# Ordered level products, decay rows written by GpSimd, and equal statistics tiles in a two-layer hybrid of attention and gated linear attention

## The chip, the cores and the metric

One core of one Trainium2 chip runs the whole kernel. The metric is device microseconds of one execution, from the first to the last instruction with the little that lies around them. Less is better.

## What is computed

Two layers, each a feed-forward block, a token mixer and a second feed-forward block, all with a root-mean-square norm before and after, over 16 meta tokens and 256 sequence tokens (272 columns) of width 1024. In the second layer the meta tokens are dropped after the mixer's keys and values.

```python
for l in range(DEPTH):
    h = h + 0.5 * rmsnorm(swiglu(rmsnorm(h, g_pre_ffn1[l]), w_ffn1_gu[l], w_ffn1_down[l]), g_post_ffn1[l])
    mix = token_mixer(rmsnorm(h, g_pre_mix[l]), ...)
    h = h + rmsnorm(mix, g_post_mix[l])
    h = h + 0.5 * rmsnorm(swiglu(rmsnorm(h, g_pre_ffn2[l]), w_ffn2_gu[l], w_ffn2_down[l]), g_post_ffn2[l])

# in the mixer, attention with a forget gate (8 heads of 64)
s = q @ k.T * scale + cum[q] - cum[k];  p = softmax(where(allowed, s, -inf));  o = p @ v
# in the mixer, gated linear attention (4 heads, keys of 64, values of 128)
att[t, s] = sum_k q[t, k] * k[s, k] * exp(cb[t, k] - cb[s, k])   # s <= t, in blocks of 128
```

Here `cum` and `cb` are running sums of log gates along the tokens.

## The kernel before, in words

Activations lie transposed: 128 partitions of features, 272 columns of tokens. Each weight block (128x1024, fetched by SyncE) is split by ScalarE (`wh`, line 106) and VectorE (`wl`, line 112) into a rounded part and a rest, and each 128x128 piece gives three products of 272 columns (`mm3`, lines 122 to 124), one after another on TensorE. These products fill the program. A scheduler that simulates the program sets the order of instructions on every engine, within the program's dependencies; the mixer spreads its small work over the 41 projection blocks by a table (`at(i, function)`).

Four places matter here.

**Statistics.** `inv_rms` (lines 164 to 186) gives one over the root mean square of every token, as a row that is the same on all 128 partitions. Squares are summed over features by products with a column of ones (line 171), tokens in tiles of 128, 128 and 16 (of 128 and 128 where meta tokens are gone); VectorE scales the sums in one operation for the full tiles and one for the rest (line 179); GpSimd raises them to the power of minus one half (line 180); TensorE turns the columns back into a row by full products with the identity (line 183). `prep` calls it while products go on: five times with 272 columns, once with 256. `Post.done` calls it between two blocks, where TensorE has nothing else: four times with 272 columns, once with 256. There 5 and then 8 products whose result nobody reads (`idle`, line 161) fill TensorE's wait.

**Decay rows.** `decays` (from line 396) makes the running sums `cf` of the eight attention heads. The scores are products of 104 rows: 64 of the head, rows 64 to 72 and 96 to 104 for the two sums, and zeros between, which GpSimd writes once a layer (lines 344 and 345). `qa` has ones marks in 64 to 72 and `cf` in 96 to 104, `ka` has `-cf` and marks; the sums come by two DMAs on ScalarE's queue (lines 421 and 422), the marks by two on GpSimd's (lines 346 and 347).

**Scores.** `scores(b)` (line 645) makes two heads' scores in two products each; `meta_scores` (line 694) those of the meta tokens.

**Level products.** Gated linear attention is summed over seven levels (64, 32, ..., 1). `level` makes decayed keys and queries `E`, `products` multiplies them per head. Heads 0 and 2 lie on partitions 0 to 63, heads 1 and 3 on 64 to 127 (`r` is the half). For levels of 16 and less a head has two products of 128 stationary columns (line 562), and in the first layer, for levels of 8 and less, a third of 16 stationary columns for the meta tokens (line 565):

```python
for hd in range(GH):
    r, hh = hd % 2, hd // 2
    x = head_rows(E, hd)
    for k in range(2):
        nc.tensor.matmul(pp[r][...], x[:, o : o + P], second(x[:, o : o + P], L), ...)
    if meta:
        nc.tensor.matmul(pp[r][:META, ...], x[:, :META], second(x[:, :META], L), ...)
```

`diagonal` (lines 588 and 590) has the same form with 128 and 16 columns. A product of 32-bit operands shows as two rows in the trace, a transposition as one.

Of the kernel before, what the change touches and what calls it, by code (L numbers as in the profile page):

```python
# [9 lines left out]
F32 = mybir.dt.float32  # L10
# [3 lines left out]
ALU = mybir.AluOpType  # L14
AX = mybir.AxisListType

P = 128
META = 16
SEQ = 256
NT = META + SEQ  # L20
D = 1024
# [27 lines left out]
def hybrid_kernel(ctx: ExitStack, tc: tile.TileContext, xT, w_in, w_al, w_fg, w_o, w_gu1, w_dn1, w_gu2, w_dn2, w_end, g_end, vecs, consts, marks, out):  # L49
# [22 lines left out]
    ms = cp.tile([P, 4], F32, name="ms")  # L72
    nc.gpsimd.memset(ms, 1.0)
# [90 lines left out]
    def inv_rms(parts, n, factor, warm=False):  # L164

        tt = [(o, min(P, n - o)) for o in range(0, n, P)]
        J = len(tt)
        st = bank("po")
        for i, part in enumerate(parts):
            for j, (o, m) in enumerate(tt):  # L170
                last = nc.tensor.matmul(st[:m, j : j + 1], part[:, o : o + m], one, start=i == 0 and j == 0,
                                 stop=i == len(parts) - 1, skip_group_check=True)
        if warm:
            idle(last, WARM[0])
        rp = sp.tile([P, 4], F32, tag="rp", name="rp")
        q = 1.0 / (factor * factor)
        for m, a, b in ((P, 0, n // P), (n % P, n // P, J)):
            if m and b > a:
                nc.vector.tensor_scalar(ms[:m, a:b], st[:m, a:b], q / D, q * EPS, ALU.mult, ALU.add)
        nc.gpsimd.tensor_tensor(rp[:, :J], ms[:, :J], nhalf[:, :J], ALU.pow)  # L180
        bc = bank("po")
        for j, (o, m) in enumerate(tt):
            last = nc.tensor.matmul(bc[:, o : o + m], rp[:m, j : j + 1].broadcast_to([m, P]), ident[:m, :m], start=True, stop=True)  # L183
# [156 lines left out]
    def operands():  # L340

        qa = cp.tile([P, FH, NT], F32, tag="qa", name="qa")
        ka = cp.tile([P, FH, NT], F32, tag="ka", name="ka")
        nc.gpsimd.memset(qa[64:96], 0.0)
        nc.gpsimd.memset(ka[64:96], 0.0)
        nc.gpsimd.dma_start(qa[64:72], marks)
        nc.gpsimd.dma_start(ka[96:104], marks)
        return qa, ka

    def mixer(l, xh, xl, rs, qa, ka, c0):  # L350
# [6 lines left out]
        with tc.tile_pool(name="mix", bufs=1) as mp, tc.tile_pool(name="tmp", bufs=2) as tp:  # L357
# [39 lines left out]
            def decays():  # L397
# [17 lines left out]
                cf = a[32:40, 2, :]  # L415
                nc.vector.tensor_tensor_scan(cf, one[32:40].broadcast_to([8, NT]), b[32:40, 2, :], 0.0, ALU.mult, ALU.add)
                for f in range(2):
                    nc.vector.tensor_tensor_scan(G[:, f, :], one.broadcast_to([P, NT]), b[:, f, :], 0.0, ALU.mult, ALU.add)
                nf = sm[32:40]
                nc.vector.tensor_scalar(nf, cf, -1.0, None, ALU.mult)  # L420
                nc.scalar.dma_start(qa[96:104], cf.unsqueeze(1).broadcast_to([8, FH, NT]))
                nc.scalar.dma_start(ka[64:72], nf.unsqueeze(1).broadcast_to([8, FH, NT]))
# [108 lines left out]

            def products(i):
# [23 lines left out]
                for hd in range(GH):  # L556
                    r, hh = hd % 2, hd // 2
                    x = head_rows(E, hd)
                    for k in range(2):
                        o = TILES[k + 1][0]  # L560
                        q = 2 * k + hh
                        nc.tensor.matmul(pp[r][:, q * 64 : q * 64 + 64].rearrange("p (b l) -> p b l", l=L), x[:, o : o + P],  # L562
                                         second(x[:, o : o + P], L), start=True, stop=True)
# [13 lines left out]
            def diagonal():  # L577
# [4 lines left out]
                for hd in range(GH):  # L582
                    r, hh = hd % 2, hd // 2
                    xk, xq = head_rows(gk, hd), head_rows(gq, hd)
                    for k in range(2):
                        o = TILES[k + 1][0]
                        q = 2 * k + hh
# [354 lines left out]
```

## Time and profile before

| what | value |
|---|---|
| median of three runs | 1270.57 us (1266.27 to 1270.88) |
| the profiled execution | 1268.24 us |
| its span, first to last instruction | 1266.4 us |
| TensorE busy | 1247.4 us, 99% |
| VectorE busy | 893.4 us, 71% |
| ScalarE busy | 697.5 us, 55% |
| GpSimd busy | 34.9 us, 3% |
| TensorE's granted clock | 0.997 of full speed |

In the trace's rows PE is TensorE, DVE is VectorE, ACT is ScalarE, POOL is GpSimd and SP is SyncE. L122 is line 122 of the kernel, `out<-in` are the program's tile names. Ends of TensorE's rows are modelled and overlap the next row, so what a product costs is read from the start of one row to the start of the next.

### The profile page before, as it was taken

The page shows a single profiled execution, that of the slowest core. Times are in us where ns is not written, and L with a number is a line of the kernel's source. Part 1 is how long each engine was busy: PE and PEld are TensorE (multiplying, and loading weights), DVE is VectorE, ACT ScalarE, POOL GpSimd, SP SyncE. Part 2 cuts the span into 40 slices and gives each one's busy share as a digit, 9 for nine tenths or more (in the row PEclk, how much of TensorE's full clock was granted, in tenths as well). Part 3 has the DMA queues.
Part 4 walks back from the last instruction along what each step waited for, and adds up shares of the span by engine and source line. Part 5 has one row for each costly group of instructions (what it writes and reads, how often), then busy time and mean ns, then how long its engine had stood idle before and what let it go on. Part 6 is the DMA issues. An engine that isn't in the chain of part 4 may idle for free.

```text
span 1266.4 us, 25250 instructions
## 1 busy us (share of the span) xinstructions
PE 1247.4 (99%) x9826; PEld 1210.2 (96%) x9826; DVE 893.4 (71%) x1831; ACT 697.5 (55%) x1451; POOL 34.9 (3%) x43
## 2 busy tenths in 40 slices
PE   7999999999999999999999999999999999999997
PEld 7999999988999999999999999999898999999986
DVE  6777655887567787776568777558986687877662
ACT  7555544764555565554446555446755554755551
POOL 2000000000000100000000000001000000000000
PEclk9999999999999999999999999999999999999999
DMA  9655555443245636556536555564434564665650
GB/s 307 203 171 170 166 175 158 153 119 100 88 138 176 178 126 184 172 170 169 177 114 212 172 178 161 168 192 134 138 96 122 161 185 155 200 187 182 181 166 34
DMA packets 58198, 203.87 MB, mean 161 GB/s; under 512 B 6688, under 2 KB 8000, under 8 KB 58048
## 3 DMA queue, kind: packets, MB, share of 16 engines
q1 hardware_dynamic: 57376, 201.19, 51.7%
q8 instruction: 77, 1.26, 0.4%
q10 hardware_dynamic: 576, 0.80, 0.3%
q14 instruction: 41, 0.34, 0.1%
q0 software_dynamic: 128, 0.28, 0.1%
HBM read 200.92 MB, written 1.05 MB: 159 GB/s over the span
## 4 chain that ended last, share of the span: by engine, by line
PE 82%; issue 14%; DMA 1%; ACT 1%; POOL 0%; SPq 0%; ACTq 0%; DVE 0%; DVEq 0%; POOLq 0%
PE mm L122 13%; PE mm L124 12%; PE mm L123 12%; PE pp L122 7%; PE pp L124 7%; PE pp L123 7%; PE s L122 5%; PE s L123 5%; PE s L124 5%; PE pp L562 1%; PE s L161 1%; PE s L645 1%; DMA w<-in_w_gu 1%; PE po L183 1%; DMA ka<-sm 1%
## 5 line engine op out<-in xcount | busy, mean ns | idle before, releaser
L106 ACT CAST wh<-w 128x512 fp32r<-128x512 f32 (+1 forms) x768 | 464.6, 613 | 414.9 <-PE mm L123 183.8
L112 DVE TENSOR_TENSOR wl<-w,wh 128x512 fp32r<-128x512 f32 (+1 forms) x768 | 516.2, 681 | 246.4 <-ACT wh L106 231.0
L122 PE MATMUL mm<-xh,wh 128*128 128x272 f32 (+1 forms) x1072 | 309.4, 291 | 9.6 <-ACT wh L106 8.7
L124 PE MATMUL mm<-xh,wl 128*128 128x272 f32 (+1 forms) x1072 | 308.8, 289 | 0.0
L123 PE MATMUL mm<-xl,wh 128*128 128x272 f32 (+1 forms) x1072 | 307.8, 288 | 0.0
L122 PEld LDWEIGHTS mm<-xh,wh 128*128 128x128 f32 x1072 | 201.7, 189 | 11.7 <-ACT wh L106 8.9
L123 PEld LDWEIGHTS mm<-xl,wh 128*128 128x128 f32 x1072 | 202.9, 189 | 1.2 <-issue 0.9
L124 PEld LDWEIGHTS mm<-xh,wl 128*128 128x128 f32 x1072 | 202.2, 189 | 1.6 <-issue 1.1
L124 PE MATMUL s<-xh,wl 128*128 128x272 f32 (+1 forms) x496 | 142.2, 287 | 0.0
L123 PE MATMUL s<-xl,wh 128*128 128x272 f32 (+1 forms) x496 | 142.0, 287 | 0.0
L122 PE MATMUL s<-xh,wh 128*128 128x272 f32 (+1 forms) x496 | 141.0, 288 | 0.0
L124 PE MATMUL pp<-xh,wl 128*128 128x272 f32 (+1 forms) x480 | 137.2, 289 | 0.0
L123 PE MATMUL pp<-xl,wh 128*128 128x272 f32 (+1 forms) x480 | 137.0, 288 | 0.0
L122 PE MATMUL pp<-xh,wh 128*128 128x272 f32 (+1 forms) x480 | 134.0, 289 | 0.0
L123 PEld LDWEIGHTS s<-xl,wh 128*128 128x128 f32 x496 | 93.4, 188 | 0.1
L124 PEld LDWEIGHTS s<-xh,wl 128*128 128x128 f32 x496 | 93.4, 188 | 0.0
L122 PEld LDWEIGHTS s<-xh,wh 128*128 128x128 f32 x496 | 92.8, 188 | 0.1
L123 PEld LDWEIGHTS pp<-xl,wh 128*128 128x128 f32 x480 | 90.9, 189 | 0.0
L124 PEld LDWEIGHTS pp<-xh,wl 128*128 128x128 f32 x480 | 90.8, 190 | 0.0
L122 PEld LDWEIGHTS pp<-xh,wh 128*128 128x128 f32 x480 | 89.3, 190 | 0.0
L122 PE MATMUL pp<-hh,wh 128*128 128x272 f32 x264 | 76.1, 288 | 0.0
L122 PE MATMUL mm<-hh,wh 128*128 128x272 f32 x264 | 76.1, 288 | 0.0
(291 smaller groups left out, 2123.9 us busy)
## 6 DMA issues: line engine op xcount, KB each, us to landing
w<-in_w_gu SPq DMA_DIRECT2D x175, 512.0 KB, 3.6
w<-in_w_in SPq DMA_DIRECT2D x82, 512.0 KB, 3.6
w<-in_w_dn SPq DMA_DIRECT2D x48, 512.0 KB, 3.5
w<-in_w_end SPq DMA_DIRECT2D x22, 512.0 KB, 4.0
w<-in_w_dn SPq DMA_DIRECT2D x24, 384.0 KB, 3.5
w<-in_w_fg SPq DMA_DIRECT2D x16, 512.0 KB, 3.6
w<-in_w_o SPq DMA_DIRECT2D x16, 512.0 KB, 3.6
h<-in_xT SPq DMA_DIRECT2D x8, 136.0 KB, 4.7
```

The costliest lines, as they stand in the source:

```text
L106: i = nc.scalar.copy(wh[:, :n], w[:, a:b])
L112: nc.vector.tensor_tensor(wl[:, :n], w[:, a:b], wh[:, :n].bitcast(F32), ALU.subtract)
L122: nc.tensor.matmul(o, a, x[0], start=start, stop=False)
L123: nc.tensor.matmul(o, a, x[1], start=False, stop=False)
L124: nc.tensor.matmul(o, b, x[0], start=False, stop=stop)
L161: m = nc.tensor.matmul(o[:, :P], ident, ident, start=True, stop=True)
L183: last = nc.tensor.matmul(bc[:, o : o + m], rp[:m, j : j + 1].broadcast_to([m, P]), ident[:m, :m], start=True, stop=True)
L562: nc.tensor.matmul(pp[r][:, q * 64 : q * 64 + 64].rearrange("p (b l) -> p b l", l=L), x[:, o : o + P], second(x[:, o : o + P], L), start=T ...
L645: nc.tensor.matmul(s[:, c : c + e], qa[:104, hd, q0:e], ka[:104, hd, 0:e], start=True, stop=True)
```

## The change

Products of all heads come first, alternating between the partition halves, the narrow meta ones last and with 128 stationary columns in place of 16 (112 of the resulting rows are not read). The running sums go into the scores once only: `ka` gets `cf` in rows 64 to 72 by a GpSimd copy out of the scan's result, `qa` has marks of minus one, and scores have 72 rows. The term of the query's own sum is left out, which a softmax along keys does not see. The zero rows, their GpSimd writes, one marks DMA, the negation on VectorE and both DMAs on ScalarE's queue go. `inv_rms` cuts 272 tokens into four tiles of 68, scales with one VectorE operation, and turns back by transpositions.

```diff
     def inv_rms(parts, n, factor, warm=False):
-        tt = [(o, min(P, n - o)) for o in range(0, n, P)]
-        J = len(tt)
+        m = P if n % P == 0 else n // 4
+        tt = range(0, n, m)
...
-        for m, a, b in ((P, 0, n // P), (n % P, n // P, J)):
-            if m and b > a:
-                nc.vector.tensor_scalar(ms[:m, a:b], st[:m, a:b], q / D, q * EPS, ALU.mult, ALU.add)
-        nc.gpsimd.tensor_tensor(rp[:, :J], ms[:, :J], nhalf[:, :J], ALU.pow)
+        nc.vector.tensor_scalar(ms[:m, :J], st[:m, :J], q / D, q * EPS, ALU.mult, ALU.add)
+        nc.gpsimd.tensor_tensor(rp[:m, :J], ms[:m, :J], nhalf[:m, :J], ALU.pow)
         bc = bank("po")
-        for j, (o, m) in enumerate(tt):
-            last = nc.tensor.matmul(bc[:, o : o + m], rp[:m, j : j + 1].broadcast_to([m, P]), ident[:m, :m], start=True, stop=True)
+        for j, o in enumerate(tt):
+            last = nc.tensor.transpose(bc[:, o : o + m], rp[:m, j : j + 1].broadcast_to([m, P]), ident[:m, :m])
...
     def operands():
-        nc.gpsimd.memset(qa[64:96], 0.0)
-        nc.gpsimd.memset(ka[64:96], 0.0)
         nc.gpsimd.dma_start(qa[64:72], marks)
-        nc.gpsimd.dma_start(ka[96:104], marks)
...
                 for rows, f0, f1 in parts:
                     nc.vector.tensor_tensor(b[rows, f0:f1, :], b[rows, f0:f1, :], a[rows, f0:f1, :], ALU.subtract)
-                cf = a[32:40, 2, :]
-                nc.vector.tensor_tensor_scan(cf, one[32:40].broadcast_to([8, NT]), b[32:40, 2, :], 0.0, ALU.mult, ALU.add)
+                    if f0 == 2:
+                        cf = a[rows, 2, :]
+                        nc.vector.tensor_tensor_scan(cf, one[rows].broadcast_to([8, NT]), b[rows, 2, :], 0.0, ALU.mult, ALU.add)
+                        nc.gpsimd.tensor_copy(ka[64:72], cf.unsqueeze(1).broadcast_to([8, FH, NT]))
...
-                nf = sm[32:40]
-                nc.vector.tensor_scalar(nf, cf, -1.0, None, ALU.mult)
-                nc.scalar.dma_start(qa[96:104], cf.unsqueeze(1).broadcast_to([8, FH, NT]))
-                nc.scalar.dma_start(ka[64:72], nf.unsqueeze(1).broadcast_to([8, FH, NT]))
...
+            def both_halves(ks):
+                return [(k, hh, r) for k in range(ks) for hh in range(2) for r in range(2)]
...
-                    if meta:
-                        nc.tensor.matmul(pp[r][:META, 256 + hh * 8 : 264 + hh * 8].rearrange("p (b l) -> p b l", l=L),
-                                         x[:, :META], second(x[:, :META], L), start=True, stop=True)
+                for _, hh, r in both_halves(meta):
+                    x = E[64 * r : 64 * r + 64, hh]
+                    nc.tensor.matmul(pp[r][:, 256 + hh * 8 : 264 + hh * 8].rearrange("p (b l) -> p b l", l=L),
+                                     x[:, :P], second(x[:, :META], L), start=True, stop=True)
...
-                        nc.tensor.matmul(s[:, c : c + e], qa[:104, hd, q0:e], ka[:104, hd, 0:e], start=True, stop=True)
+                        nc.tensor.matmul(s[:, c : c + e], qa[:72, hd, q0:e], ka[:72, hd, 0:e], start=True, stop=True)
```

How the scheduler's order moves is shown at three places; a row's `x2` is two instructions of that form. First TensorE at a level's products in the first layer (the level of 1; `E_4141` are its operands, `pp_4194` and `pp_4195` the banks of the two halves), before:

```order
L124 MATMUL mm_4155<-xh_2755,wl_4073 128x272
L562 MATMUL pp_4194<-E_4141 128x64 x2
L565 MATMUL pp_4194<-E_4141 16x8
L562 MATMUL pp_4195<-E_4141 128x64 x2
L565 MATMUL pp_4195<-E_4141 16x8
```

and the end of the same level now:

```order
L558 MATMUL pp_4194<-E_4141 128x64
L558 MATMUL pp_4195<-E_4141 128x64
L562 MATMUL pp_4194<-E_4141 128x8
L562 MATMUL pp_4195<-E_4141 128x8
...
L120 MATMUL mm_4221<-xh_2755,wh_4133 128x272
L121 MATMUL mm_4221<-xl_2756,wh_4133 128x272
```

The two pairs of rows came twice before, a narrow product behind every two wide ones of a head; now eight wide ones come in alternation and four narrow ones behind them.

Second, GpSimd from the statistics before the first layer's mixer to the mixer's end (`rp` are powers in `inv_rms`, `ss` powers of the mixer's own norm), before:

```order
L443 MEMSET vm_3002 128x32
L180 TENSOR_TENSOR rp_2736<-ms_73,nhalf_75 128x3
L180 TENSOR_TENSOR rp_2824<-ms_73,nhalf_75 128x3
L748 TENSOR_TENSOR ss_4415<-ss_4415,nhalf_75 16x4
L748 TENSOR_TENSOR ss_4518<-ss_4518,nhalf_75 128x4
```

and now:

```order
L436 MEMSET vm_3004 128x32
L177 TENSOR_TENSOR rp_2736<-ms_2735,nhalf_73 68x4
L177 TENSOR_TENSOR rp_2826<-ms_2825,nhalf_73 68x4
L413 COPY ka_155<-lsa_3072 8x2176
L744 TENSOR_TENSOR ss_4415<-ss_4415,nhalf_73 16x4
L744 TENSOR_TENSOR ss_4518<-ss_4518,nhalf_73 128x4
```

The copy of 2176 elements a partition stands between the powers; the next operation in GpSimd's queue belongs to the mixer's end.

Third, TensorE at the first two heads' scores in the first layer (`mm_3333` is the block of values of heads 2 and 3, `mm_3390` the block behind it), before:

```order
L122 MATMUL mm_3333<-xh_2755,wh_3234 128x272
L123 MATMUL mm_3333<-xl_2756,wh_3234 128x272
L124 MATMUL mm_3333<-xh_2755,wl_3235 128x272
L645 MATMUL s_3254<-ka_155,qa_154 128x144
L645 MATMUL s_3254<-ka_155,qa_154 128x272
L645 MATMUL s_3261<-ka_155,qa_154 128x144
L645 MATMUL s_3261<-ka_155,qa_154 128x272
L122 MATMUL mm_3333<-xh_2755,wh_3238 128x272
```

and now:

```order
L122 MATMUL mm_3390<-xh_2755,wl_3309 128x272
L545 MATMUL pp_3378<-E_3327 64x64 x2
L545 MATMUL pp_3379<-E_3327 64x64 x2
L641 MATMUL s_3254<-ka_155,qa_154 128x144
L641 MATMUL s_3254<-ka_155,qa_154 128x272
L641 MATMUL s_3261<-ka_155,qa_154 128x144
L641 MATMUL s_3261<-ka_155,qa_154 128x272
```

The scores stood in the middle of the block `mm_3333`, after 68 products of 272 columns behind the decays' own (line 402); now they stand after 102 of them, behind the next block and inside the products of the level of 64.

## Rows read from the trace of the kernel before

**Rows 1.** The page, busy time of each engine: busy us (share of the span) xinstructions.

```profile
PE 1247.4 (99%) x9826; PEld 1210.2 (96%) x9826; DVE 893.4 (71%) x1831; ACT 697.5 (55%) x1451; POOL 34.9 (3%) x43
```

**Rows 2.** Timeline of PE, a level's products, first layer: start, us, what.

```profile
325.08 0.29 PE L124 MATMUL mm<-xh,wl 128*128 128x272 f32 x1
325.30 0.66 PE L562 MATMUL pp<-E 64*128 64x64 f32 x4
325.89 0.20 PE L565 MATMUL pp<-E 64*16 64x8 f32 x2
...
328.41 0.28 PE L123 MATMUL mm<-xl,wh 128*128 128x272 f32 x1
```

**Rows 3.** Timeline of PE, a level's products, second layer.

```profile
917.31 0.29 PE L124 MATMUL mm<-xh,wl 128*128 128x272 f32 x1
917.53 1.16 PE L562 MATMUL pp<-E 64*128 64x64 f32 x16
...
918.84 0.28 PE L123 MATMUL mm<-xl,wh 128*128 128x256 f32 x1
```

**Rows 4.** Timeline of PE, the diagonal's products, first layer, then second.

```profile
331.18 0.29 PE L124 MATMUL mm<-xh,wl 128*128 128x272 f32 x1
...
334.75 0.29 PE L123 MATMUL mm<-xl,wh 128*128 128x272 f32 x1
...
963.03 0.28 PE L124 MATMUL mm<-xh,wl 128*128 128x256 f32 x1
...
964.66 0.28 PE L123 MATMUL mm<-xl,wh 128*128 128x256 f32 x1
```

**Rows 5.** Timeline of PE, statistics inside running products: sums, then the turning back.

```profile
20.30 0.29 PE L122 MATMUL mm<-xh,wh 128*128 128x272 f32 x1
...
21.21 0.29 PE L124 MATMUL mm<-xh,wl 128*128 128x272 f32 x1
...
24.60 0.29 PE L124 MATMUL pp<-xh,wl 128*128 128x272 f32 x1
...
25.81 0.29 PE L123 MATMUL pp<-xl,wh 128*128 128x272 f32 x1
```

**Rows 6.** Timeline of all engines, between two blocks: sums scaled, power, turning back.

```profile
650.43 0.21 DVE L179 TENSOR_SCALAR ms<-po 128x2 f32<-128x2 f32 x2 [0.37 <-PE po L171]
650.81 0.85 POOL L180 TENSOR_TENSOR rp<-ms,nhalf 128x3 f32<-128x3 f32 x1 [186.76 <-DVE ms L179]
...
651.72 1.03 PE L183 MATMUL po<-con,rp 128*128 128x128 f32 x6
...
652.68 2.05 PE L161 MATMUL s<-con 128*128 128x128 f32 x16
```

**Rows 7.** Groups by line: shapes xcount, busy us, mean ns, idle before.

```profile
L748 POOL TENSOR_TENSOR ss<-ss,nhalf 128x4 f32<-128x4 f32 x4 | 4.0, 1007 | 125.3 <-DVE ss L747 125.3
L345 POOL MEMSET ka<- 32x2176 f32 x2 | 3.8, 1912 | 52.3 <-PE pp L124 52.3
```

**Rows 8.** Waits of PE: who, for whom, us in total, times, longest.

```profile
PE s L645 <- DMA ka<-sm: 2.1, 2, 1.1
PE mm L122 <- DVE ka L436: 0.9, 2, 0.6
```

**Rows 9.** Timeline of DVE at the first layer's decays.

```profile
248.43 0.71 DVE L416 TENSOR_TENSOR_SCAN lsa<-ones,lsb 8x272 f32<-8x272 f32 x1
...
249.93 0.29 DVE L420 TENSOR_SCALAR sm<-lsa 8x272 f32<-8x272 f32 x1
...
251.78 1.34 DVE L418 TENSOR_TENSOR_SCAN G<-ones,lsb 128x272 f32<-128x272 f32 x2
```

**Rows 10.** Busy us of each engine, 250 to 260 us.

```profile
250.00:260.00 10.00, 8.62 (x63) 7.93 (x61) 9.84 (x25) 6.86 (x16) 0.00 (x0) 1.00 0.54 164
```

**Rows 11.** Timeline of DVE and POOL where a power meets subtractions.

```profile
232.49 1.87 DVE L112 TENSOR_TENSOR wl<-w,wh 128x512 fp32r<-128x512 f32 x3
232.70 2.38 POOL L180 TENSOR_TENSOR rp<-ms,nhalf 128x3 f32<-128x3 f32 x1 [16.95 <-DVE ms L179]
```

More of the change, by code (lines that the diff above doesn't have):

```diff
@@ L71, in hybrid_kernel @@
     one = ones[:, 0:1]
-    ms = cp.tile([P, 4], F32, name="ms")
-    nc.gpsimd.memset(ms, 1.0)
     nhalf = cp.tile([P, 4], F32, name="nhalf")
@@ L555, in products @@
                 mask = con[:, C_LVL + i * P : C_LVL + (i + 1) * P].bitcast(I32)
[L556 to L563, printed above, removed]
-                    if meta:
-                        nc.tensor.matmul(pp[r][:META, 256 + hh * 8 : 264 + hh * 8].rearrange("p (b l) -> p b l", l=L),
-                                         x[:, :META], second(x[:, :META], L), start=True, stop=True)
+                for k, hh, r in both_halves(2):
+                    x = E[64 * r : 64 * r + 64, hh]
+                    o = TILES[k + 1][0]
+                    q = 2 * k + hh
+                    nc.tensor.matmul(pp[r][:, q * 64 : q * 64 + 64].rearrange("p (b l) -> p b l", l=L), x[:, o : o + P],
+                                     second(x[:, o : o + P], L), start=True, stop=True)
+                for _, hh, r in both_halves(meta):
+                    x = E[64 * r : 64 * r + 64, hh]
+                    nc.tensor.matmul(pp[r][:, 256 + hh * 8 : 264 + hh * 8].rearrange("p (b l) -> p b l", l=L),
+                                     x[:, :P], second(x[:, :META], L), start=True, stop=True)
                 for r in range(2):
@@ L581, in diagonal @@
                 mask = con[:, C_LVL + i * P : C_LVL + (i + 1) * P].bitcast(I32)
[L582 to L587, printed above, removed]
-                        nc.tensor.matmul(pp[r][:, q * P : (q + 1) * P], xk[:, o : o + P], xq[:, o : o + P], start=True, stop=True)
-                    if not c0:
-                        nc.tensor.matmul(p0[r][:META, hh * META : (hh + 1) * META], xk[:, :META], xq[:, :META], start=True, stop=True)
+                for k, hh, r in both_halves(2):
+                    xk, xq = gk[64 * r : 64 * r + 64, hh], gq[64 * r : 64 * r + 64, hh]
+                    o = TILES[k + 1][0]
+                    q = 2 * k + hh
+                    nc.tensor.matmul(pp[r][:, q * P : (q + 1) * P], xk[:, o : o + P], xq[:, o : o + P], start=True, stop=True)
+                for _, hh, r in both_halves(not c0):
+                    xk, xq = gk[64 * r : 64 * r + 64, hh], gq[64 * r : 64 * r + 64, hh]
+                    nc.tensor.matmul(p0[r][:, hh * META : (hh + 1) * META], xk[:, :P], xq[:, :META], start=True, stop=True)
                 for r in range(2):
@@ L693, in meta_scores @@
                 for hd in range(FH):
-                    nc.tensor.matmul(s[:, hd, :], qa[:104, hd, :META], ka[:104, hd, :META], start=True, stop=True)
+                    nc.tensor.matmul(s[:, hd, :], qa[:72, hd, :META], ka[:72, hd, :META], start=True, stop=True)
                 one_mask = cmask[:META, 144:160].unsqueeze(1).broadcast_to([META, FH, META])
@@ L925, in pack @@
         "consts": constants(),
-        "marks": np.ascontiguousarray(np.broadcast_to(np.eye(FH, dtype=np.float32)[:, :, None], (FH, FH, NT))),
+        "marks": np.ascontiguousarray(np.broadcast_to(-np.eye(FH, dtype=np.float32)[:, :, None], (FH, FH, NT))),
     }
```

7 lines of the change are left out of this document (4 added, 3 removed).

## Prediction

> **What bounds the kernel now.** I read the busy times of the page first. TensorE is busy 1247.4 of 1266.4 us, VectorE 71%, ScalarE 55%, GpSimd 3% [rows 1]. So TensorE sets the time almost everywhere: a step that TensorE is spared is won unless another engine is late at that place, and one that another engine is spared is worth nothing unless TensorE waits for it. 9826 rows in 1247.4 us make .127 us a row, which is the step of a 272-column product, since these fill the program; 256 columns get 256/272 of that, .12. Next I read TensorE's timeline at the places that the diff rewrites: a stretch of small products costs the time from the last big product ahead of it to the first behind it, less the big ones between. Last come the waits of TensorE at the decays [rows 8] and what VectorE does there [rows 9, 10], because there alone the change touches a place where TensorE waits.
>
> The sum is made against the profiled execution, 1268.24 us (its span and 1.84 around it). That lies 2.3 below the median of the runs shown and 2.0 above the fastest. 0.5% is 6.3 us, about what a measurement of this kernel can tell from no change; the line between "faster" and "same" is therefore 1261.9.
>
> **Level products and diagonal.** In the first layer a level costs 328.41 - 325.08 - 2 x .127 = 3.08 us [rows 2], in the second, without meta tokens, 918.84 - 917.31 - 2 x .12 = 1.29 [rows 3]. The reader is to see that the sixteen wide rows of the second layer run in one block of 1.16 us, under .08 each, while in the first the narrow ones break them into blocks of four at .66, .165 each. A row of 128 stationary columns alone takes (2.05 - .29)/15 = .117, by the sixteen idle ones [rows 6], the last one's run-out taken off as .29. So the wide rows of the second layer run two at a time, one on each half, and those of the first don't. With the change the first layer has the second's block and eight narrow rows behind it, also 128 stationary columns on alternate halves. Two at a time these cost 4 x .115 = .46 (bounds: nothing, if they hide in the run-out of the block, and .92, if one at a time). I take .46, since they have the form of the rows that pair. Per level 1.29 + .46 - 3.08 = -1.33; four levels (8, 4, 2, 1) give -5.3.
>
> The diagonal is the same: 334.75 - 331.18 - .25 = 3.32 in the first layer, 964.66 - 963.03 - .24 = 1.39 in the second [rows 4]; 1.39 + .46 - 3.32 = -1.47. Levels of 16 and more, and the second layer, only get another order of the same rows: nothing. Together **-6.8**. What this moves forward is VectorE's work on the results; by the page VectorE has 29% of the span free, but see the fourth rival.
>
> **Scores of 72 rows.** A row's step goes by its columns, and 104 or 72 partitions are one pass: nothing either way. That the scores stand 34 big products (4.3 us) later adds no step to TensorE.
>
> **Statistics inside products.** The sums of 272 columns are six rows, the narrow tile's two among them, and cost 21.21 - 20.30 - .25 = .66, .11 each [rows 5]. Four tiles of 68 make eight rows. Their price is between .11 (as now) and 68/128 of it, .06; two rows of 16 stationary columns cost far less than two of 128 [rows 2], so I go by columns: 8 x .0625 = .50, or -.16 (upper bound .88, +.22). Turning back costs 25.81 - 24.60 - .25 = .96 [rows 5] for six rows; four transpositions of one row each cost 4 x .115 = .46, or -.50. Five calls: 5 x -.66 = -3.3. The call with 256 columns goes from four rows to two, -.2.
>
> **Statistics between blocks.** Here TensorE waits for the chain sums, VectorE, GpSimd, turning back [rows 6], so each link counts. VectorE does one operation in place of two that take .21 together: -.07. The power of four columns takes 1.007 where that of three takes .85 [rows 6, 7]: +.155. From the first full product to the first filler pass 652.68 - 651.72 = .96; four transpositions and the change of form make some .55: -.41. The sums give -.05. That is -.37 a call, -1.5 for four, and -.2 for the one of 256 columns. Both kinds of statistics: **-5.2**.
>
> **Decay rows.** Taken away are two DMA issues on ScalarE's queue, a marks DMA on GpSimd's, four writes of zeros of 1.912 us [rows 7] on a GpSimd that idles, and the negation of .29 on VectorE [rows 9]. TensorE waits 2.1 us for the DMA into `ka` and .9 for VectorE at the values' copy behind it, over both layers [rows 8], so at most 3.0 is to be won. But in that stretch VectorE is busy 9.84 of 10 us and TensorE 8.62 [rows 10]. VectorE is the bound there, and with the scores later TensorE comes to the bank that it must free all the earlier and waits for that instead. So I count what VectorE wins or loses, and nothing of the 3.0.
>
> It wins the negation, .29 a layer. It can lose by the copy. The copy writes 8 x 2176 elements: no shorter than the memset with as many a partition, 1.912 [rows 7], and up to twice that, 3.8, if reading costs what writing does. Whether GpSimd and VectorE get into each other's way shows in one place: a power took 2.38 us beside subtractions of two SBUF operands, .85 elsewhere [rows 6, 11]; it lost 1.53. The scan that the copy reads ends at 248.43 + .71 = 249.14 [rows 9]; with 1.53 for the subtractions ahead and 1.91 the copy ends at 252.58. The two G scans, also of two SBUF operands, would start at 251.78 - .29 = 251.49, and lose 1.09 if they must wait for its end (nothing if no VectorE operation ever waits for GpSimd, which no row shows; 3.0 with a copy of 3.8). For two layers 2 x (1.09 - .29) = **+1.6**, with -3.0 (no blocking, all waits gone) and 2 x (3.0 - .29) = +5.4 as its ends. I take the short copy, as the memset is the only GpSimd row of such size. [...]
>
> Behind the copy GpSimd has nothing queued until the power at the mixer's end, some 90 us later. The scores waited at most 1.1 us for the DMA [rows 8] and now come 4.3 us later, so what writes `ka` may be done 3.2 us later than that DMA at no cost to them.
>
> **Sum.** -6.8 - 5.2 + 1.6 = -10.4: 1268.24 - 10.4 = 1257.8, forecast as **1258 us** (own range 1255 to 1260.5).
>
> **Rivals.**
> 1. *The copy takes 3.8 us and holds the G scans for all of it*: +5.4 instead of +1.6, 1261.6. For it: the late power, and a VectorE without slack. Against: the first scan could have been served before the copy. Chance .13.
> 2. *No blocking, and the waits go*: -3.0 instead of +1.6, 1253.2. For it: the waits are in the trace, and their cause (a DMA, a late copy of values) is removed or moved away. Against: VectorE's 9.84 of 10. Chance .13.
> 3. *Narrow rows don't do what they should*: the meta rows go one at a time (+.46 five times, 2.3) and 68 stationary columns cost like 128 (+.38 nine times, 3.4): 1258 + 5.7, 1263.5. For it: no row shows eight stationary-wide, eight-column products behind a block, or 68 columns. Against: rows of 16 columns are cheap. Chance .10.
> 4. *VectorE becomes the bound through the levels*: half of the 6.8 comes back as waits for level operands or banks, +3.4: 1261.2. For it: VectorE is full at the decays [rows 10], and the levels follow directly. Against: by rows 1 it has 29% of the span free. Chance .10.
> 5. *Slower: the copy is an element-by-element one*. Its source is broadcast eight times; if GpSimd takes c us, a layer loses 249.14 + 1.53 + c - 251.49 - .29 = c - 1.11 at the G scans, and two layers eat the 12.0 of the other parts from c = 7.1 on, 3.7 times the memset. At 5 ns an element c is 10.9 and the sum is 2 x 9.8 - 12.0 = +7.6: 1275.8. For it: GpSimd is slow at powers (.155 us a column). Against: its memset takes .88 ns an element. Chance .04.
>
> **How the numbers follow.** Forecast .50 and rivals .13, .13, .10, .10, .04. The range leaves out the last alone: from rival 2, 1253.2, to rival 3, 1263.5, and 2.3 more on either side for how executions lie about the profiled one: **1251 to 1266**. Faster by over 0.5%: forecast .50, rival 2 .13, and half each of rivals 1 and 4, which lie just inside the line, .12: .75. Same: the other halves .11, rival 3 .10: .21. Slower: rival 5, .04.
>
> **What would show it.** A level of 8 to 1 in the first layer costs some 1.75 us beside its big products, not 3.08; the diagonal 1.85. In the statistics inside products the turning back takes .46, the sums .5. Between blocks the power takes 1.0 and the turning back .55. GpSimd's copy takes 1.9 to 3.8 us soon after the scan, and the G scans begin when it ends, or their own durations grow. TensorE's wait for the DMA into `ka` is gone, and a wait of like size for VectorE's work on a later bank stands in its place. The forecast is wrong if the levels keep their blocks of four, if a copy row over 7 us stands at the decays, or if new waits of several us appear between the levels.

## The result, and the profile after

The changed kernel takes 1257.26 us (median of four, 1255.99 to 1258.45), the kernel before 1268.93: ratio 0.9908, 95% interval 0.9888 to 0.9928. The forecast was 1258 and faster. The profiled execution went from 1268.24 to 1256.44, by -11.8 where the sum said -10.4. The total came out nearly right, but several of its terms were off and cancelled.

The page's busy line of the kernel after, against [rows 1]: TensorE has the same number of rows but for four, and 14.6 us less of them.

```profile
PE 1232.8 (98%) x9830; PEld 1199.3 (96%) x9830; DVE 895.1 (71%) x1820; ACT 697.0 (56%) x1451; POOL 33.2 (3%) x38
```

To find the place of every microsecond I used the products of the weights. There are 8792 of them in each trace, the same ones in every stage (some 290 of them change places inside a stage), so the start of the n-th in one trace can be set against the start of the n-th in the other. A stage runs from one such product to another; the borders are the 65th, 113th, 1801st, 2261st, 6301st, 6761st and last (20.98, 28.07, 249.36, 350.80, 887.59, 978.28 and 1257.28 us in the kernel before). What a stage gained or lost against the kernel before, in us:

| stage | forecast | measured |
|---|---|---|
| start, to the 65th product | 0 | -3.20 |
| first statistics | -0.66 | +1.24 |
| next pair of statistics (between blocks, in products) | -1.03 | -1.34 |
| first layer's mixer (levels, diagonal, decays) | -6.0 | -5.15 |
| three more pairs of statistics | -3.1 | -4.18 |
| second layer's mixer | +0.8 | +1.26 |
| the rest, 256 columns | -0.4 | -0.50 |
| sum | -10.4 | -11.87 |

**Levels and diagonal.** TensorE's timeline after, at the level of 1 and at the diagonal of the first layer:

```profile
319.74 0.29 PE L122 MATMUL mm<-xh,wl 128*128 128x272 f32 x1
319.96 1.11 PE L558 MATMUL pp<-E 64*128 64x64 f32 x16
320.90 0.56 PE L562 MATMUL pp<-E 64*128 64x8 f32 x8
...
321.63 0.29 PE L121 MATMUL mm<-xl,wh 128*128 128x272 f32 x1
...
324.39 0.29 PE L122 MATMUL mm<-xh,wl 128*128 128x272 f32 x1
324.61 1.16 PE L583 MATMUL pp<-gq,gk 64*128 64x128 f32 x16
325.61 0.52 PE L586 MATMUL s<-gq,gk 64*128 64x16 f32 x8
...
326.29 0.29 PE L121 MATMUL mm<-xl,wh 128*128 128x272 f32 x1
```

The sixteen wide rows stand in one block of 1.11 us, where [rows 2] shows blocks of four at 0.66. The level costs 321.63 - 319.74 - 0.25 = 1.64 us (forecast 1.75, before 3.08), the diagonal 326.29 - 324.39 - 0.25 = 1.65 (forecast 1.85, before 3.32). Over the whole first mixer the time from each row's start to the next adds up, by kind, to:

```
                                 before   after
wide level rows (x80)             10.98    4.95
narrow meta rows of levels (x32)   2.16    2.29
diagonal, both kinds (x24)         3.11    1.45
products of weights (x460)        63.22   65.92
scores (x48)                       5.30    5.82
```

So the rows of levels and diagonal are 7.6 us shorter here (6.03 - 0.13 + 1.66), and the steps from one big product to the next, waits among them, are 2.7 longer. That is the decays.

**Decays.** VectorE and GpSimd after, at the first layer's decays (against [rows 9, 10]):

```profile
246.12 0.72 DVE L409 TENSOR_TENSOR lsb<-lsb,lsa 128x544 f32<-128x544 f32 x1
246.76 2.48 DVE L110 TENSOR_TENSOR wl<-w,wh 128x512 fp32r<-128x512 f32 x1
249.17 0.88 DVE L429 TENSOR_TENSOR ka<-mm,rs 64x272 f32<-64x272 f32 x2
250.08 1.34 DVE L415 TENSOR_TENSOR_SCAN G<-ones,lsb 128x272 f32<-128x272 f32 x2
...
246.26 2.44 POOL L413 COPY ka<-lsa 8x2176 f32<-8x2176 f32 x1 [14.83 <-DVE lsa L412]
```

The copy's row starts at 246.26, while VectorE's subtraction of two SBUF operands runs to 246.84. It ends at 248.70, 1.86 us after that. The next subtraction, which takes 0.69 elsewhere, takes 2.48 and ends half a microsecond behind the copy. VectorE stood still for 1.79 us. In the second layer the copy meets the G scans, which take 2.22 together instead of 1.34:

```profile
879.67 0.69 DVE L110 TENSOR_TENSOR wl<-w,wh 128x512 fp32r<-128x512 f32 x1
880.28 0.88 DVE L429 TENSOR_TENSOR ka<-mm,rs 64x272 f32<-64x272 f32 x2
881.20 2.22 DVE L415 TENSOR_TENSOR_SCAN G<-ones,lsb 128x272 f32<-128x272 f32 x2
...
879.80 2.42 POOL L413 COPY ka<-lsa 8x2176 f32<-8x2176 f32 x1 [15.50 <-DVE lsa L412]
```

Here too it ends 1.86 us behind the subtraction that runs when its row starts (882.22 against 880.36), so I read the row's first part as a wait.

The waits of TensorE after (against [rows 8]) are those for VectorE's work, as the forecast said, and the one for the DMA is gone:

```profile
PE mm L120 <- DVE qa L431: 2.4, 1, 2.4
PE mm L120 <- DVE ka L429: 2.4, 2, 1.8
```

What I had not forecast is the clock. It stands in the busy time by window (PE, PEld, DVE, ACT, POOL, then the granted clock, the DMA share and GB/s):

```profile
250.00:252.00 2.00, 1.80 (x12) 1.83 (x13) 1.97 (x5) 0.18 (x1) 0.00 (x0) 0.83 0.00 0
252.00:254.00 2.00, 2.00 (x11) 2.00 (x11) 1.97 (x7) 0.69 (x2) 0.00 (x0) 0.50 0.47 68
254.00:256.00 2.00, 1.96 (x13) 1.74 (x13) 1.96 (x5) 1.49 (x3) 0.00 (x0) 0.81 0.48 195
```

Behind its wait of 1.84 us, which ends at 250.20, TensorE's granted clock fell to 0.50 for about 3.4 us. The big products there start 0.227 us apart and not 0.126; that is 1.6 us more. The kernel before has no such stretch here. It is not a loss of its own, though: behind the slow stretch, at 255.02, TensorE comes to a bank of results that VectorE's copy of the queries (`qa`) leaves free only at 254.87, so at full clock it would have waited there (the run with two marks DMAs, below, does). In the second layer TensorE does wait there, for 2.40 us, and the clock stays at 1.00:

```profile
886.98 0.36 PE L120 MATMUL mm<-xh,wh 128*128 128x272 f32 x1 [2.40 <-DVE qa L431]
...
888.00:890.00 2.00, 2.00 (x18) 2.00 (x17) 1.97 (x7) 1.03 (x3) 0.00 (x0) 1.00 0.60 174
```

**Statistics.** Between two blocks after, at the same place as [rows 6]:

```profile
640.58 0.16 DVE L176 TENSOR_SCALAR ms<-po 68x4 f32<-68x4 f32 x1 [0.28 <-PE po L169]
640.81 1.00 POOL L177 TENSOR_TENSOR rp<-ms,nhalf 68x4 f32<-68x4 f32 x1 [185.68 <-DVE ms L176]
...
641.87 0.45 PE L180 MATMUL po<-con,rp 68*128 68x68 f32 x4 [0.18 <-POOL rp L177]
...
642.16 1.55 PE L159 MATMUL s<-con 128*128 128x128 f32 x12
```

The power takes the forecast 1.0; from the first row of the turning back to the fillers it is 0.29 and not the forecast 0.55 (before 0.96).

**Start.** Two things that the forecast did not have, of opposite sign. Busy time by window, the kernel before:

```profile
12.00:16.00 4.00, 2.13 (x18) 1.91 (x16) 1.66 (x5) 0.83 (x4) 0.00 (x0) 1.00 1.05 242
16.00:20.00 4.00, 3.35 (x13) 3.12 (x14) 3.37 (x8) 3.62 (x8) 0.00 (x0) 0.58 1.01 407
```

and after:

```profile
12.00:16.00 4.00, 4.00 (x32) 4.00 (x32) 4.00 (x10) 3.66 (x9) 0.00 (x0) 1.00 1.02 416
...
20.00:24.00 4.00, 2.76 (x23) 2.54 (x21) 3.05 (x6) 1.48 (x3) 3.96 (x1) 1.00 1.03 407
```

Before, the transfers thin out to 242 GB/s while the DMA engines stay full, TensorE is without weights at 14 us, waits 2.52 us for one, and its clock is at 0.58 from 16 to 20 us. After, 416 GB/s come through and the gap is gone. But VectorE now has seven subtractions in a row, and the first power, 4.97 us long, ends only behind them:

```profile
18.75 4.29 DVE L110 TENSOR_TENSOR wl<-w,wh 128x512 fp32r<-128x512 f32 x7
...
18.99 4.97 POOL L177 TENSOR_TENSOR rp<-ms,nhalf 68x4 f32<-68x4 f32 x1 [16.42 <-ACT wh L104]
...
24.01 0.45 PE L180 MATMUL po<-con,rp 68*128 68x68 f32 x4 [1.25 <-POOL rp L177]
```

### The profile page after: what moved, and what is told of

The parts are those of the page before. It is cut to its first block, busy times and chain, and to the rows that moved or that the text cites. A ratio compares the mean times of both kernels' runs of the same rounds, so it can differ in the third digit from the quotient of the medians.

```text
span 1254.4 us, 25215 instructions
## 1 busy us (share of the span) xinstructions
PE 1232.8 (98%) x9830; PEld 1199.3 (96%) x9830; DVE 895.1 (71%) x1820; ACT 697.0 (56%) x1451; POOL 33.2 (3%) x38
## 3 DMA queue, kind: packets, MB, share of 16 engines
q8 instruction: 77, 1.26, 0.4%
## 4 chain that ended last, share of the span: by engine, by line
PE 81%; issue 15%; DMA 1%; POOL 1%; DVE 1%; ACT 1%; SPq 0%; DVEq 0%; POOLq 0%; ACTq 0%
PE mm L120 13%; PE mm L121 12%; PE mm L122 12%; PE pp L121 7%; PE pp L120 7%; PE pp L122 7%; PE s L121 5%; PE s L122 5%; PE s L120 5%; PE s L641 1%; PE pp L558 1%; PE s L159 1%; POOL rp L177 1%; DMA w<-in_w_gu 1%; PE po L738 1%
## 5 line engine op out<-in xcount | busy, mean ns | idle before, releaser
L120 PEld LDWEIGHTS mm<-xh,wh 128*128 128x128 f32 x1072 | 202.2, 190 | 15.3 <-ACT wh L104 7.5
```

The source lines that it names most:

```text
L120: nc.tensor.matmul(o, a, x[0], start=start, stop=False)
```

## The experiments

Theory after the result: levels, diagonal and statistics land on TensorE in full; GpSimd's copy stops VectorE's work on two SBUF operands for its length (1.86 us), and TensorE pays by a wait and, I thought, a second time by the clock behind it (two marks DMAs answers that); the shorter start comes from the marks and zero writes. For each run, what the stages gained or lost against the kernel before (from one profiled execution each, in us; the starts of the last five, which are alike there, lie 0.5 apart):

| kernel | start | first stat. | next pair | mixer 1 | three pairs | mixer 2 | rest | sum |
|---|---|---|---|---|---|---|---|---|
| the change | -3.20 | +1.24 | -1.34 | -5.15 | -4.18 | +1.26 | -0.50 | -11.9 |
| levels alone | -0.73 | +0.01 | -0.02 | -6.11 | -0.01 | -0.37 | +0.02 | -7.2 |
| statistics alone | -0.22 | -0.68 | -1.36 | -0.62 | -4.20 | +6.51 | -0.44 | -1.0 |
| decay rows alone | -4.41 | +0.56 | -0.03 | +4.59 | +0.01 | +3.91 | -0.02 | +4.6 |
| copy on ScalarE | -3.62 | -0.22 | -1.36 | -6.81 | -4.22 | -0.90 | -0.36 | -17.5 |
| marks put back | -0.69 | -0.68 | -1.37 | -5.14 | -4.20 | +1.25 | -0.44 | -11.3 |
| two marks DMAs | -3.00 | -0.20 | -1.35 | -5.15 | -4.19 | +2.77 | -0.42 | -11.5 |
| copy twice | -3.36 | +1.23 | -1.35 | +3.37 | -4.20 | +5.82 | -0.46 | +1.1 |
| late marks | -3.58 | -0.70 | -1.37 | -6.81 | -4.26 | -0.91 | -0.36 | -18.0 |
| narrow last | -3.78 | -0.70 | -1.35 | -7.62 | -4.28 | -0.90 | -0.44 | -19.1 |
| wide in place | -4.00 | -0.70 | -1.35 | -4.81 | -4.28 | -0.66 | -0.44 | -16.2 |
| old levels | -3.71 | -0.70 | -1.38 | +8.31 | -4.27 | -0.63 | -0.36 | -2.7 |
| no transposition | -4.10 | -0.08 | -0.10 | -7.66 | +1.04 | -1.07 | +0.10 | -11.9 |

### The three parts, each alone

The first two are the hunks of the diff on `products` and `diagonal`, and on `inv_rms`; the third is all the rest.

**Levels alone.**

> The kernel before with only the level and diagonal products rewritten. Theory (TensorE is the bound, all of it lands): about 6.9 us less than before, ratio 0.9946; each level of 8, 4, 2, 1 in the first layer 1.3 to 1.45 us less, the diagonal 1.5 to 1.7 less. Rival (VectorE takes it back as waits): half, 3.4 us less, ratio 0.997.

Measured: 1260.62 against 1269.77, ratio 0.9926 (0.9897 to 0.9955): 9.2 less by the medians, 7.2 in the profiled executions, where 6.9 was expected. The first mixer gains 6.11 us, the second 0.37, and nothing is lost elsewhere; the rows of levels and diagonal are 6.5 us shorter in the first mixer. TensorE has no wait there that the kernel before has not: VectorE takes nothing back.

**Statistics alone.**

> The kernel before with only the equal statistics tiles and transpositions. Theory: 5.2 to 6.0 us less than before, ratio 0.995 to 0.996; inside products 0.66 to 0.85 a call, between blocks 0.37 to 0.55 a call. Rival (the price is the eight rows of sums, or the power of four columns waits longer): 2 us less, ratio 0.998.

Measured: 1267.86 against 1269.77, ratio 0.9985 (0.997 to 1.0), less than expected. The statistics themselves gain all they should (-0.68, -1.36, -4.20, -0.44 in the table). The second mixer loses 6.51 to something else. The waits and one window of this kernel:

```profile
PE s L642 <- DMA ka<-sm: 3.8, 2, 3.4
...
894.00:898.00 4.00, 4.00 (x18) 3.60 (x17) 2.86 (x12) 0.41 (x2) 0.00 (x0) 0.57 0.51 188
```

The old DMA into `ka` is here 3.4 us late for the scores (1.1 at most in [rows 8]), and the clock falls behind it. It leaves later because the negation that it reads now stands on VectorE behind the G scans, 3.7 us later in the stage; the kernel before has it ahead of them, as in [rows 9]:

```profile
886.75 1.34 DVE L415 TENSOR_TENSOR_SCAN G<-ones,lsb 128x272 f32<-128x272 f32 x2
...
888.70 0.29 DVE L417 TENSOR_SCALAR sm<-lsa 8x272 f32<-8x272 f32 x1
```

So the old decays could cost as much as the new ones, depending on the order that the scheduler gave.

**Decay rows alone.**

> The kernel before with only the decay rows and 72-row scores. Theory (GpSimd's copy holds VectorE's two-operand work for its whole length, 1.9 us, less what was removed): 1 to 3 us MORE than before, ratio 1.001 to 1.0025, with one VectorE row near the decays stretched by 1 to 1.8 us. Rival (the waits for the DMA go and nothing replaces them): 3 us less, ratio 0.9976.

Measured: 1274.47, ratio 1.0038 (1.0022 to 1.0055): slower, as the theory said and the rival did not, and by more than it said. The mixers lose 4.59 and 3.91, the start gains 4.41. In both layers the subtraction beside the copy takes 2.49 in place of 0.69, as the theory said. In the first mixer the clock is at 0.61 from 303 to 306, behind a level in the old form, and at 0.66 from 318 to 322; TensorE is busy all the time there. In the second it falls behind a wait of 1.93 us.

The three do not add up (-7.2 - 1.0 + 4.6 = -3.6 against -11.9). Of the 6.5 us that the statistics alone lost in the second mixer about 4.2 (2.5 of wait, 1.7 of clock) belong to the DMA that the decay rows take away, and what the decay rows alone lost in the first one is less when the levels are in the new order.

### The copy

**Copy on ScalarE.**

```diff
-nc.gpsimd.tensor_copy(ka[64:72], cf.unsqueeze(1).broadcast_to([8, FH, NT]))
+nc.scalar.copy(ka[64:72], cf.unsqueeze(1).broadcast_to([8, FH, NT]))
```

> The changed kernel with the copy on ScalarE in place of GpSimd. Theory (the copy's price is that it stops VectorE): the stretched subtraction returns from 2.48 to 0.69 us and the stretched G scan from 1.61 to 0.67, the program is 1 to 2.5 us faster than the changed one, about 1255. Rival 1 (the loss at the decays comes from the later place of the scores): no faster than the changed one, 1257. Rival 2 (ScalarE, which makes the weights, has no room for 2 us a layer): up to 4 us slower, 1261.

Measured: 1251.56, ratio 0.9856 (0.9832 to 0.9881); 5.7 us less than the changed kernel, more than the expected 1 to 2.5. ScalarE's copy, and VectorE's rows beside it:

```profile
244.29 2.01 ACT L413 COPY ka<-lsa 8x2176 f32<-8x2176 f32 x1 [0.17 <-DVE lsa L412]
...
244.88 0.69 DVE L110 TENSOR_TENSOR wl<-w,wh 128x512 fp32r<-128x512 f32 x1
...
246.39 1.34 DVE L415 TENSOR_TENSOR_SCAN G<-ones,lsb 128x272 f32<-128x272 f32 x2
```

The copy is no shorter, but the subtraction is back at 0.69 and the scans at 1.34. The granted clock stays at 1.00 through both mixers. Against the changed kernel the mixers gain 1.66 and 2.16: GpSimd's copy costs 3.8 us of TensorE's time. The scheduler also puts the scores earlier in this kernel, so this is the price of the copy with the place of the scores that goes with it. The other 1.9 us come from the start and the first statistics, where the first power takes 1.35 in this run, in between the subtractions.

**Copy twice.** GpSimd's line stands twice.

> The changed kernel with GpSimd's copy made twice. Theory (the copy holds VectorE's work of two SBUF operands, 1.86 us each): VectorE rows at the decays are stretched by up to twice 1.86, TensorE waits 1.5 to 3.7 us more over both layers. Rival (only the first start blocks, or VectorE gets in between the two): no more than 0.5 us more; the second copy is late instead.

Measured: one time, 1269.24, 12.8 more than the changed kernel's profiled execution. GpSimd's copies and the scans of the second layer, and one window of the first:

```profile
888.14 2.42 POOL L413 COPY ka<-lsa 8x2176 f32<-8x2176 f32 x1 [15.50 <-DVE lsa L412]
890.62 2.32 POOL L414 COPY ka<-lsa 8x2176 f32<-8x2176 f32 x1
...
889.54 3.98 DVE L416 TENSOR_TENSOR_SCAN G<-ones,lsb 128x272 f32<-128x272 f32 x2
...
312.00:318.00 6.00, 5.95 (x26) 5.21 (x26) 3.13 (x9) 1.76 (x8) 0.00 (x0) 0.50 0.31 87
```

Each copy stops one scan: 3.98 for the two, where one copy made 2.22 and none 1.34. That agrees with the theory's mechanism, and so does TensorE: its waits for VectorE's `ka` and `qa` grow from 4.8 to 7.5 us, by 2.7, inside the expected 1.5 to 3.7. The total is far more, because most of the loss is the clock: it is at 0.50 from 312 to 322 and from 896 to 902, and some 17 us more at half clock than in the changed kernel are 8.5 us of work. The stretch at 312 lies 60 us behind the stopped scans, where the scheduler has put the small products of several levels together; how much of it is the copy's and how much the new order's stays open.

### The start

**Marks put back.**

```diff
     def operands():
+        nc.gpsimd.memset(qa[64:96], 0.0)
+        nc.gpsimd.memset(ka[64:96], 0.0)
         nc.gpsimd.dma_start(qa[64:72], marks)
+        nc.gpsimd.dma_start(ka[96:104], marks)
```

> The changed kernel with the zero writes and the second marks DMA of the kernel before put back on GpSimd (nobody reads them). Theory, formed on the traces: the changed kernel's first 21 us are shorter because its marks DMA leaves before the weights' and is only one; put back, weight transfers thin out at 10 to 16 us, TensorE waits 2 to 3 us for a weight at about 14 us as before, and the program is 2 to 3.5 us slower than the changed one, about 1260. Rival (the start's difference is scatter between executions): as the changed one, 1257.

Measured: 1257.33, ratio 0.9907 (0.989 to 0.9924), as the changed kernel; the expected total was wrong. Yet the expected mechanism is in the trace:

```profile
12.00:16.00 4.00, 2.24 (x18) 2.02 (x17) 1.75 (x6) 1.55 (x4) 0.00 (x0) 1.00 1.04 262
16.00:20.00 4.00, 3.79 (x20) 3.57 (x20) 3.83 (x8) 2.92 (x8) 0.00 (x0) 0.57 1.03 413
```

The gap and the low clock of the kernel before are back, and the start loses 2.5 us. The first statistics win 1.9 of it back: the first power takes 1.34 and not 4.97.

**Two marks DMAs.** Only the last line of that diff.

> The changed kernel with the second marks DMA alone put back, without zero writes, so both leave at about 2 to 3 us. If the number of marks DMAs costs the time: TensorE's wait at 14 us comes back, 1 to 3 us. If their place in time does (behind 4 us of zero writes, among the weights): no wait, the first 21 us as in the changed kernel within 0.5.

Measured: one time, 1256.7, with a start of -3.00. So it is the place in time that costs, behind 4 us of zero writes and among the first weights, not the number; what the zero writes would cost alone no run shows. The first power took 2.56 here.

This execution also prices the half clock. In its first layer TensorE waits 1.85 us for `ka`, as in the changed kernel, but the clock stays at 1.00, and it then waits for `qa`; in its second layer the clock falls behind a wait of 2.41, where it stayed up in the changed kernel:

```profile
253.77 0.36 PE L120 MATMUL mm<-xh,wh 128*128 128x272 f32 x1 [1.56 <-DVE qa L432]
...
252.00:254.00 2.00, 0.44 (x4) 0.26 (x3) 1.93 (x6) 1.93 (x4) 0.00 (x0) 1.00 0.63 231
...
886.00:888.00 2.00, 2.00 (x12) 2.00 (x11) 1.97 (x6) 0.00 (x0) 0.00 (x0) 0.53 0.35 33
```

The first mixer stands at -5.15 in both kernels: there VectorE's lateness is what is paid, and the half clock only fills the time up to the next bank. In the second layer TensorE comes to no such wait behind it, and the mixer loses 1.5 us more (2.77 against 1.26).

**Late marks.** The copy on ScalarE and, in place of the marks DMA in `operands`, in `mixer`:

```diff
             nc.sync.dma_start(wal, w_al[l])
+            nc.sync.dma_start(qa[64:72], marks)
```

> The copy on ScalarE, and the marks DMA of each layer on SyncE's queue behind the first weights in place of GpSimd's at the start. If the one marks DMA left still costs at the start: 0.5 to 1.5 us less than with the copy on ScalarE alone, about 1250.5. If not: the same, 1251.5 within 0.5; if it delays a weight that it stands ahead of: up to 1 us more.

Measured: 1250.23, ratio 0.9848 (0.9832 to 0.9865). The start is that of the copy on ScalarE (-3.58); the gain of 0.5 in the profiled executions stands in the first statistics. By the profile the DMA that was left did not cost at the start. By the medians this kernel gains 1.3, which is the size expected if it did; where the other 0.8 lies no trace shows.

### Levels: order or width

All four start from late marks.

**Narrow last.** The meta products last as in the change, but 16 stationary columns wide (`x[:, :META]`, `xk[:, :META]`).

> The fastest kernel so far (copy on ScalarE, marks late; 1250.2) with the meta products last as now, but 16 stationary columns wide again. If the 128 columns make the gain: 2 to 5 us slower, 1252 to 1255. If the order makes it (theory): the four narrow products of a level cost 0.2 to 0.5 us as the wide ones do, total within 1 us of 1250.2.

Measured: 1248.73, ratio 0.9834 (0.9815 to 0.9854): the fastest of all, 1.5 less than late marks, where within 1 was expected.

```profile
314.37 1.11 PE L558 MATMUL pp<-E 64*128 64x64 f32 x16
315.41 0.26 PE L562 MATMUL pp<-E 64*16 64x8 f32 x8
```

Behind a block of wide rows the narrow ones cost 1.12 us in all four levels, against 2.49 with 128 columns. The widening loses 1.4 us there; of it 0.8 is left in the first mixer as a whole (-7.62 against -6.81), since other small products have longer steps.

**Wide in place.** The order of before, the meta products 128 columns wide.

> The same kernel with the order of before (head by head, the meta product behind each head's two), but the meta products 128 stationary columns wide. If the order makes the gain (theory): the wide rows of the first layer cost 0.13 to 0.14 us again in place of 0.06 to 0.07, 6 to 8 us slower, 1256 to 1258. If the width makes it: within 1.5 us of 1250.2.

Measured: 1252.26, ratio 0.9868 (0.9845 to 0.989), 2.0 more than late marks and 4 to 6 less than expected. The wide rows of the levels cost 7.25 us against 5.86, not the 11 of before. The theory that the order alone makes the gain falls: one narrow product between wide ones is what costs, and either remedy takes most of it away. The second layer, which has no narrow ones, agrees: its 80 wide rows cost 6.22 us in the old order and 6.37 in the new.

**Old levels.** Levels and diagonal wholly as before.

> The same kernel with levels and diagonal wholly as before. Theory: 6 to 8 us slower, 1256 to 1258, as wide_in_place within 1 us. Rival (part of the alternate order's worth is that TensorE's clock stays up behind the level products, as it did not in the kernel with the decay rows alone): 8 to 11 us, with a granted clock of 0.5 in a stretch behind a level.

Measured: 1259.03, ratio 0.9921 (0.9893 to 0.9949); 8.8 more than late marks, the rival's range. Its executions lie between 1256.99 and 1265.53, and the profiled one is the slowest. There the clock fell four times in the first mixer:

```profile
322.00:326.00 4.00, 4.00 (x33) 3.56 (x32) 2.75 (x6) 2.66 (x5) 0.00 (x0) 0.97 0.39 135
326.00:330.00 4.00, 4.00 (x20) 3.86 (x20) 1.22 (x4) 0.53 (x1) 0.00 (x0) 0.50 0.38 131
```

TensorE shows no wait here: up to 325.5 it runs the blocks of four of a level. So of the 15.3 us that this execution's table line stands behind late marks, the wide rows have 6.1, the diagonal 1.8, and 7.3 stand in slower big products.

**No transposition.** Four equal tiles, turned back by full products.

> The same kernel with four equal tiles, but turned back by full products in place of transpositions: eight rows a call in place of four. Theory: 0.4 to 0.5 us a call for nine calls and 0.2 for two, 4 to 5 us slower, 1254 to 1255. Rival (eight narrow rows run as cheaply as four, or hide in the wait for the power): within 1 us.

Measured: 1256.26, ratio 0.9893 (0.9868 to 0.9919); 6.0 more, above the expected 4 to 5. A pair of statistics costs 1.27 more (-0.10 against -1.37), 0.6 to 0.7 a call. On top of it, between blocks ahead of the second mixer:

```profile
845.74 1.44 PE L180 MATMUL po<-con,rp 68*128 68x68 f32 x8 [0.28 <-POOL rp L177]
...
846.00:848.00 2.00, 2.00 (x13) 2.00 (x13) 0.74 (x2) 0.00 (x0) 0.00 (x0) 0.59 0.00 0
```

the clock fell once behind the longer turning back.

## Why the prediction was right, and where its steps were not

**Levels and diagonal: right, a little too small.** Forecast -6.8, by rows -7.6 in the changed kernel and -6.5 with the levels alone. A level came to 1.64 and not 1.75, the diagonal to 1.65 and not 1.85: the eight meta rows add 0.35 us to the 1.29 of the second layer and 0.26 to its 1.39, where the forecast had .46. That is below the .46 of rows two at a time and far below the .92 of rows one at a time; the third rival is out. But the step "they have the form of the rows that pair" missed that 16 columns behind the block are cheaper still.

**Scores of 72 rows: as forecast.** From a score row of 144 columns to the next score row it is 0.12 us, from one of 272 columns 0.23, with 104 partitions before and with 72 after. The half microsecond that the sums by kind have more for scores (5.82 against 5.30) lies where they border on other products.

**Statistics: right in sign, mis-sized.** Forecast -5.2; without the first call, which has a story of its own, -4.5 against a measured -6.0 (-1.34 - 4.18 - 0.50). The term that was too small is the turning back: a transposition in place of a full product is worth 0.6 to 0.7 a call, where I had 0.41 to 0.50. The equal tiles, with their sums and the longer power, add about 0.1 a pair.

**Decays: mechanism right, price too low.** Against the kernel before they cost 2.6 us if the levels are worth what they won alone (the two mixers' -5.15 + 1.26, less -6.11 - 0.37), and 3.7 by the rows of the changed kernel (with 7.6 for the levels); I had 1.6. The forecast said that VectorE is the bound there, that the copy may hold its work on two SBUF operands, and that the waits of [rows 8] come back under another name; all three stand in the trace. (The wait that it puts to the values' copy behind the scores is for the keys of the heads, `ka`, ahead of them.) The durations were near: the copy runs 1.86 us (forecast 1.91), it waited 0.58 for VectorE (forecast 1.53), and VectorE lost 1.79 + 0.88 - 0.58 = 2.1 (forecast 1.6), in the first layer at a subtraction and only in the second at the G scans.

The step that came short is "So I count what VectorE wins or loses". TensorE's waits grew by more than that: in the first layer at full clock (two marks DMAs) they are 1.85 and 1.56 us, before 0.25 and 1.13; in the second (the changed kernel) 0.51 and 2.40, before 0.60 and 0.94. That is 3.4 in place of VectorE's 2.1. The forecast had seen why without giving it a price: before, TensorE did the first scores ahead of the bank of `qa`, and now they stand behind it, so it "comes to the bank that it must free all the earlier" and waits longer. That this makes the whole of the difference is not shown, since no run moves the scores alone. The half clock behind the first wait, which looks like the cause, cost the changed kernel nothing that the next wait would not have cost.

With the copy on ScalarE, and the scores earlier, the mixers are 3.8 us shorter, so the price hangs on GpSimd's copy and the order that goes with it. The second rival (no blocking) is out. The first (a copy of 3.8) is out by its mechanism.

The forecast's +1.6 rests on GpSimd's copy holding VectorE, which no row of the kernel before shows ([rows 11] have the other direction). The changed kernel shows it: VectorE stood still beside the copy (2.48 against 0.69). Not all of its work did: the operations with a PSUM operand beside the second layer's copy keep their 0.44 each (L429 above), and a subtraction beside a zero write in the kernel before keeps its 0.69:

```profile
418.83 1.92 POOL L345 MEMSET ka<- 32x2176 f32 x1 [52.32 <-PE pp L124]
...
419.34 0.69 DVE L112 TENSOR_TENSOR wl<-w,wh 128x512 fp32r<-128x512 f32 x1
```

**Start: missed.** "Four writes of zeros ... on a GpSimd that idles" and a marks DMA were costed at nothing. GpSimd does idle, but its DMAs left after the zero writes (at 5.70 and 6.39 us), among the first weights, and TensorE waits for a weight behind that (2.52 us, up to 16.65). Leaving both out is worth -2.5 us at the start (marks put back). The first power's 4.97 us took 1.9 back. Together the start and the first statistics stand at -2.0 where the forecast had -0.7. This -1.3, with -0.8 of the levels (by rows) and -1.5 of the statistics, outweighed the 2.1 that the decays cost more. That the sum came within 1.5 us is in part luck: its terms were off by more and cancelled.

**Fourth rival:** VectorE does not become the bound through the levels; levels alone won 6.5 us in the two mixers with no new wait. **Fifth:** the copy took 1.86 us and not over 7, or .85 ns an element; the 5 ns that this rival supposes stand in no row.

## What to carry to other kernels

A stage in which two engines are both near full is priced by TensorE's waits, not by the busy time won or lost beside it (here 3.4 us against 2.1): follow TensorE from bank to bank in the new order, work that has moved behind a bank included. Price a stretch at half clock by whether TensorE would have waited at its end: in the first mixer it would, and the stretch cost nothing (-5.15 with it and without); in the second it would not, and the mixer lost 1.5 us more (2.77 against 1.26). Before work goes to an engine that idles, look what runs beside it: here GpSimd's copy held a subtraction of VectorE for 1.79 us, and ScalarE, with more to do, was the better place for it by 3.8 us, the order that came with it included. Don't put a narrow product between wide ones on TensorE (0.14 us a wide row, against 0.06 in a block of their own); and compare two traces by the starts of the products that they have in common, since a total hides terms that cancel.

## What the runs showed of the hardware

- Beside GpSimd's copy of 1.86 us VectorE's work on two SBUF operands stood still: a subtraction took 2.48 us in place of 0.69 (first layer of the changed kernel) and two G scans 2.22 in place of 1.34 (second layer). With the copy made twice the two scans took 3.98. Operations with a PSUM operand kept their 0.44 beside it. Beside ScalarE's copy of 2.01 us the subtraction kept its 0.69.
- The first power took 4.97 us beside a run of seven subtractions of 4.29 us (changed kernel), and 1.35 beside a run of seven of 4.53 us (copy on ScalarE). It took 4.97 with the copy made twice and 2.56 with two marks DMAs. What decides it is open.
- TensorE's granted clock fell to 0.50 behind some waits and not behind others as long: behind 1.84 us in the first layer of the changed kernel, not behind 1.85 and 1.56 with two marks DMAs; behind 2.41 in the second layer with two marks DMAs, not behind 2.40 in the changed kernel. It fell behind 3.4 us (statistics alone) and 2.5 us for a weight (before, at 14 us), and stayed at 1.00 behind 1.1 us at the decays of the kernel before [rows 8]. It also fell with TensorE busy throughout, behind levels in the old form (0.50 from 326 to 330 us in old levels, 0.61 from 303 to 306 in decay rows alone). What decides is open.
- Rows of 64 partitions and 128 stationary columns cost 0.06 to 0.08 us each in a block of their own, in either order of the halves (4.95 us for 80 in the changed kernel's first layer; 6.22 and 6.37 for 80 in the second layer, old order and new). With a product of 16 columns behind every two products they cost 0.14 (10.98 for 80, kernel before), with one of 128 there only 0.09 (7.25 for 80, wide in place).
